# Decoder trunk with SwiGLU FFNs: the weight sums of the first FFN queued behind the latest activation split, and the second block's weight split queued behind the first block's copy

## The chip, the cores and the metric

The kernel runs on one core of a Trainium2 chip. The metric is the time of one execution on the device, in microseconds (us). The time before is the median of three runs, 1953.83 us (1948.05 to 1954.03). A profiled execution gives the trace from which all durations below come; its times are those of that one execution.

## What is computed

The reference is a decoder trunk of two layers on 512 tokens (T) of width 1024 (D). Each layer is a "macaron": half a feed-forward network (FFN), a token mixer (a short convolution in the first layer, sparse attention in the second), and another half FFN. That makes four FFNs. Cut to the part that the change touches:

```python
def swiglu(h, w_in, w_out):                 # h 512x1024, w_in 1024x(2*2816), w_out 2816x1024
    g, u = jnp.split(h @ w_in, 2, axis=-1)
    return (jax.nn.silu(g) * u) @ w_out

def adaln(x, g, shift, scale):
    return rms_norm(x, g) * (1 + scale[:, None, :]) + shift[:, None, :]

for i in range(DEPTH):
    mod = (cond @ ada_w[i] + ada_b[i]).reshape(bsz, 3, 3, D_MODEL)
    shift, scl, gate = mod[:, :, 0], mod[:, :, 1], mod[:, :, 2]
    h = adaln(x, norm_g[i, 0], shift[:, 0], scl[:, 0])
    x = x + HALF * gate[:, 0, None, :] * swiglu(h, ffn_w_in[i, 0], ffn_w_out[i, 0])
    ...
    h = adaln(x, norm_g[i, 2], shift[:, 2], scl[:, 2])
    x = x + HALF * gate[:, 2, None, :] * swiglu(h, ffn_w_in[i, 1], ffn_w_out[i, 1])
```

The products of the FFN are the bulk of the work. All data are float32.

## The kernel before

**A product in three.** TensorE multiplies in a shortened float32 form, so every operand is kept as two parts, high and low. `split` (L162) makes them: ScalarE copies the raw operand into the high part (L163), and VectorE subtracts that from the raw one to give the low part (L164). A product `mm3` is then three matmuls: high by high (L167), high weights by low data (L168 in the trace's names with `tl` or `hlo`), low weights by high data (L169, with `qal`, `wlo` and so on). A weight is usable when both its ScalarE copy and its VectorE subtraction are done, and each stands in the queue of its engine, which works in order.

**Seven products for eight.** The 2816 hidden units of an FFN are 22 blocks of 128, in four groups (`FOUR`: blocks 0 to 5, 6 to 11, 12 to 17, 18 to 21). For most blocks gate and up are computed together by `seven_products(j)`: a scheme that takes seven products of half size instead of eight, on sums of weight quarters and sums of data quarters. Each of the seven is 12 matmuls of 128x256. On TensorE a block reads its weights in this order: `a11` (tiles `whi`, `wlo`), then the `b4` product of the block before (`qdh`, `qdl`), `a12` (`whi`, `wlo`), `b2` (`qbh`, `qbl`), `s1` (`qah`, `qal`), the last product of the block before (`qch`, `qcl`), `s3` (`qah`, `qal`). The first block of a group has no block before it: `a11`, `a12`, `b2`, `s1`, `s3`. In the first FFN blocks 6 to 21 go this way (groups two to four), in the other three FFNs blocks 3 to 21.

**Where a block's weights come from.** Two loads by SyncE's queue (L647, L648) fill the halves of `qa`; an accumulating transfer of GpSimd's queue (L654) adds a third quarter to both. SyncE then loads `wraw` (L656) and `a22` (L657). VectorE forms the *weight sums*: L661 adds half of `wraw` to half of `qa`, L662 adds the other half of `wraw` to that; these give `qb` and so `b2` and `b4`. Then `split` makes `whi`/`wlo` from `wraw`, `qah`/`qal` from `qa`, and `qbh`/`qbl` from the first sum. In the first FFN there are two buffers for `qa`, three for `wraw`, `whi` and `wlo`, and one each for `qah`, `qal`, `qbh`, `qbl` and the rest; a load into a buffer waits until its last reader is done.

**After a product.** ScalarE copies the first three results out of PSUM into `e` and `e3` (L696, with raised priority); VectorE adds later products to them (L704, L713, L717); ScalarE applies Silu (L718); VectorE multiplies (L723, L724) to give the hidden activations `af`, and `split` makes `ahi` and `alo` of these. `hid.done` is the pair of instructions of the latest such split.

**Between groups.** After each group but an FFN's last, eight output projections (`y`) are added to `x` by VectorE (L804). In the first three FFNs VectorE also works through jobs for later sub-layers there: a row sum of the conditioning matrix (L147, on `adaraw`), whose 512 KB rows are loaded by GpSimd's queue (L153) or SyncE's. Some of these still stand in VectorE's queue when TensorE begins the next group.

**What sets the order.** Instructions are traced in the order of the code, and a scheduler orders each engine's queue by a priority that follows this order. Three context managers change it: `tc.high_priority()` moves an instruction forward, `behind(act, dve)` puts the instructions traced in it behind a given ScalarE and a given VectorE instruction of their queues, and `tc.issue_after(i)` puts them behind instruction `i`. A moved instruction keeps all that it waits for by data.

Of the kernel before, what the change touches and what calls it, by code (L numbers as in the profile page):

```python
# [16 lines left out]
AF = mybir.ActivationFunctionType  # L17
# [36 lines left out]
def decoder_kernel(ctx, tc, xT, cT, ng, adaw, adab, ffi, ffo, cwi, cw, cwo,  # L54
                   nwi, nwv, pos, w1, w2, qg, kg, nwo, rb, onehot, rowok, out):
    nc = tc.nc
# [20 lines left out]
    def psum(name, tag="mm"):  # L77
        tag = next(six) if tag == "mm" else {"pr": "o"}.get(tag, tag)
        return ps.tile([P, T], F32, name=name, tag=tag, bufs=2)
# [4 lines left out]
    def tmp(name, n=T, tag="t"):  # L84
        bufs, size = TAGS[tag]
        return tp.tile([P, n], F32, name=name, tag=tag, padded_shape=[P, size], bufs=bufs)
# [75 lines left out]
    def split(src, hi, lo):  # L162
        act = nc.scalar.activation(hi, src, AF.Copy)  # L163
        return act, nc.vector.tensor_tensor(lo, src, hi, ALU.subtract)  # L164

    def mm3(o, sh, sl, mh, ml, first, last, **kw):
        nc.tensor.matmul(o, sh, mh, start=first, stop=False, **kw)  # L167
        nc.tensor.matmul(o, sh, ml, start=False, stop=False, **kw)  # L168
        nc.tensor.matmul(o, sl, mh, start=False, stop=last, **kw)  # L169
# [61 lines left out]
    @contextmanager  # L231
    def behind(act, dve):
        with tc.issue_after(act.ins), tc.issue_after(dve.ins):
            yield
# [223 lines left out]
    class Hidden:  # L458
# [4 lines left out]
        def keep(self, af):  # L463
            hi = self.fa.tile([P, T], F32R, name="ahi", tag="a")
            lo = self.fa.tile([P, T], F32R, name="alo", tag="a")
            self.done = split(af, hi, lo)
            self.hi.append(hi)
            self.lo.append(lo)
# [151 lines left out]
    def ffn(s, f, nrm, nxt, w0, ahead, extra=(), soon=()):  # L620
        with ExitStack() as es:
            first = s == 0
# [5 lines left out]
            hid = Hidden(es, 12)  # L628
            keep = hid.keep
            nj = FOUR[0][1] if first else 2  # L630

            def seven_products(j, later, before):
                QT = KD * P // 2
                quart = lambda c, k: ffi[f, j, c].rearrange("p k n -> p (k n)")[:, k * QT:(k + 1) * QT]
                raw = wp.tile([P, 2, QT], F32, name="wraw", tag="wraw", bufs=3)
                whi = wp.tile([P, 2, QT], F32R, name="whi", tag="whi", bufs=3)
                wlo = wp.tile([P, 2, QT], F32R, name="wlo", tag="wlo", bufs=3)
                qa = next(sums)()  # L640
                a22 = tp.tile([P, T], F32, name="a22", tag="nacc", bufs=1) if j == nj and not first else tmp("a22")
                qb = [tmp("qb", tag="sq") for _ in range(2)] if first else swa.tile([P, 2, QT], F32, name="qb")
                qbs = qb if first else [qb[:, 0], qb[:, 1]]
                ah_, al_ = (sw.tile([P, 2, QT], F32R, name=f"qa{e}") for e in "hl")
                b2 = [sw.tile([P, QT], F32R, name=f"qb{e}") for e in "hl"]
                halves = qa if isinstance(qa, list) else [qa[:, 0], qa[:, 1]]
                nc.sync.dma_start(halves[0], quart(0, 0))  # L647
                nc.sync.dma_start(halves[1], quart(1, 1))  # L648
                a21 = quart(1, 0)
                if qa is halves:  # L650
                    for q in qa:
                        nc.gpsimd.dma_start(q, a21, accum_op=ALU.add)
                else:
                    nc.gpsimd.dma_start(qa, bass.AP(tensor=a21.tensor, offset=a21.offset, ap=[a21.ap[0], [0, 2], a21.ap[1]]),  # L654
                                        accum_op=ALU.add)
                nc.sync.dma_start(raw.rearrange("p a b -> p (a b)"), ffi[f, j, 0].rearrange("p k n -> p (k n)"))  # L656
                nc.sync.dma_start(a22, quart(1, 1))  # L657

                def operands(after):
                    with after():  # L660
                        nc.vector.tensor_tensor(qbs[0], halves[1], raw[:, 0], ALU.add)  # L661
                        nc.vector.tensor_tensor(qbs[1], qbs[0], raw[:, 1], ALU.add)  # L662
                    split(raw, whi, wlo)
                    if qa is halves:
                        for n, q in enumerate(qa):
                            split(q, ah_[:, n], al_[:, n])
                    else:
                        split(qa, ah_, al_)
                    split(qbs[0], *b2)

                if j == nj and first:
                    with behind(*held_back):
                        operands(nullcontext)
                elif later:
                    with behind(*hid.done):
                        operands(nullcontext)
                else:
                    operands((lambda: behind(*nrm.done[1])) if j == nj else nullcontext)

                def product(o, w, b, begin=True):  # L680
                    for i in range(KD // 2):
                        c = slice(i * P, (i + 1) * P)
                        mh, ml = b(i)
                        mm3(o, w[0][:, c], w[1][:, c], mh, ml, begin and i == 0, i == KD // 2 - 1, skip_group_check=True)

                a11, a12 = [(whi[:, i], wlo[:, i]) for i in range(2)]
                s3, s1 = [(ah_[:, i], al_[:, i]) for i in range(2)]
                t1, t2, t3, t4 = nrm.blocks
                lo, hi = slice(0, HT), slice(HT, T)
                ox, oy, oz = psum("gu"), psum("gu"), psum("gu")  # L690
                e = sw.tile([P, 2, HT], F32, name="e", bufs=2)
                e3 = tmp("e3", HT, "xr")

                def copied(to, o):
                    with tc.high_priority():
                        nc.scalar.activation(to, o[:, lo], AF.Copy)  # L696

                product(ox[:, lo], a11, nrm.quarter(0, 0))
                copied(e[:, 0], ox)
                before[0]()  # L700
                b4 = [sw.tile([P, QT], F32R, name=f"qd{e}") for e in "hl"]
                split(qbs[1], *b4)
                product(oz[:, lo], a12, nrm.quarter(1, 0))
                nc.vector.tensor_tensor(e[:, 0], oz[:, lo], e[:, 0], ALU.add)  # L704
                product(ox[:, lo], b2, t2, begin=False)
                copied(e[:, 1], ox)
                product(oy[:, lo], s1, t1)
                copied(e3, oy)
                before[1]()
                c22 = [sw.tile([P, QT], F32R, name=f"qc{e}") for e in "hl"]  # L710
                split(a22, *c22)
                product(ox[:, lo], s3, t3, begin=False)
                nc.vector.tensor_tensor(e3, ox[:, lo], e3, ALU.add)  # L713

                def fourth():
                    product(oy[:, lo], b4, nrm.quarter(1, 1), begin=False)
                    nc.vector.tensor_tensor(e[:, 1], oy[:, lo], e[:, 1], ALU.add)  # L717
                    nc.scalar.activation(e, e, AF.Silu)  # L718

                def last():  # L720
                    product(ox[:, lo], c22, t4, begin=False)
                    af = tmp("af")
                    nc.vector.scalar_tensor_tensor(af[:, hi], e[:, 1], -1.0, e3, op0=ALU.mult, op1=ALU.mult)  # L723
                    nc.vector.scalar_tensor_tensor(af[:, lo], e[:, 0], -1.0, ox[:, lo], op0=ALU.mult, op1=ALU.mult)  # L724
                    keep(af)

                return fourth, last

            js = [(j, c) for j in range(nj) for c in range(2)]
            shift(pool(es, "gap", 1, side="right"), 448)  # L730
# [7 lines left out]
            else:  # L738
                with ExitStack() as tf_es:
                    nrm.alloc_seven(hp, pool(tf_es, "tf", 1))  # L740
                    h = nrm.hi, nrm.lo
                    with ExitStack() as hw_es:
# [4 lines left out]
                        to = [tt.tile([P, D], F32R, name="w" + e, tag=f"t{e}1") for e in "hl"]  # L747
# [11 lines left out]
            if not first:  # L759
                for j in range(nj):  # L760
                    hid.activate(os[2 * j], os[2 * j + 1])
            held_back = []
            for p, (j0, j1) in enumerate(FOUR):
                rest = none = (lambda: None,) * 2
                for j in range(max(j0, nj), j1):
                    rest = seven_products(j, p and j == j0, rest)
                n = j1 - j0
                final = p == len(FOUR) - 1
                rest[0]()
# [11 lines left out]
                if not final:  # L781
                    begun = []
                    for d in range(KD):
                        if d < 2 and both:
# [11 lines left out]
                            w, o = begun[d]  # L796
                            project(o, w, 0, a, [(n - 1, n - 1)], False, True)
                        else:
# [3 lines left out]
                            o = psum("y")  # L802
# [10 lines left out]
            for i, d in enumerate(range(0, KD, 2)):  # L813
                if i < 2:
                    ws.append(ffn_out(f, d, 2, j0, j1))
                else:
                    t = (2, 0)[i - 2]
                    to = [tt.tile([P, KD // 2, HT], F32R, name=f"t{e}{t}").rearrange("p a b -> p (a b)") for e in "hl"]
                    raw = (own if first or i == 2 else quarter[0])().rearrange("p a b -> p (a b)")
# [18 lines left out]
            for d, t in [(d, 0) for d in range(6, KD)] + [(d, HT) for d in range(KD)]:  # L838
                o = psum("ty")
# [764 lines left out]
```

## Time and profile before

| what | value |
|---|---|
| median of the runs | 1953.83 us |
| the profiled execution | 1963.74 us |
| its span on the core | 1962.0 us |
| mean granted clock of TensorE | 0.990 |
| first FFN | about 19 to 412 us of the span |
| convolution mixer | 412 to 595 |
| second and third FFN | 600 to 941, 950 to 1290 |
| sparse attention | 1290 to 1620 |
| fourth FFN | 1630 to 1960 |

A page of the profile gives the busy time of each engine (PE is TensorE's matmuls, PEld its weight loads, DVE VectorE, ACT ScalarE, POOL GpSimd, SP SyncE), the span in slices, the transfers, and the chain of work that ended last. Views of the trace add to it: a timeline has one instruction a row (start, duration, engine, line, operation, out<-in, shapes; in brackets how long the engine stood idle before it and what ended that), the list of waits adds these up by what was waited for, and a table of windows gives busy times and the clock granted to TensorE in a stretch. A row's duration includes the end of a pipeline that overlaps the next instruction, so the spacing of two rows is often shorter than the first one's duration.

### The profile page before, as it was taken

To read this page: it belongs to the slowest core of one execution; us is meant where nothing else is said; L and a number is where in the kernel's file an instruction comes from. 1 tells how busy PE (TensorE), PEld (TensorE's weight loads), DVE (VectorE), ACT (ScalarE), POOL (GpSimd) and SP (SyncE) were. 2 spreads that over 40 slices of the span, in tenths; PEclk is the share of its full clock that TensorE was granted. 3 is DMA by queue.
4 is the path that set the end of the run, shared out by engine and by line. 5 is a ranking of instruction groups with operands and counts; after the bars stand their busy time and mean duration, and the time that the engine had idled before them with its cause. 6 is when DMAs were issued, how large, how long until landed. Compare 5 with 4: busy or idle time off the path is not lost.

```text
span 1962.0 us, 34451 instructions
## 1 busy us (share of the span) xinstructions
PE 1893.6 (97%) x13293; PEld 1756.4 (90%) x13293; DVE 1520.0 (77%) x2792; ACT 958.9 (49%) x1679; POOL 250.1 (13%) x346
## 2 busy tenths in 40 slices
PE   7998989899999999999999999999999999999999
PEld 5988888898889998989989898999989789898989
DVE  8966757679789787877968777788798988675765
ACT  3334343443226353535635353555688867363532
POOL 0010101000011111110011111000245531000100
PEclk9998999999999999999999999999999999999999
DMA  9575657528665676774377677324233324664741
GB/s 331 184 219 148 204 149 207 182 82 279 212 235 134 205 207 206 208 220 138 111 209 202 203 200 213 126 80 143 73 104 83 93 65 119 168 165 135 193 120 65
DMA packets 126673, 324.76 MB, mean 166 GB/s; under 512 B 15515, under 2 KB 16651, under 8 KB 126508
## 3 DMA queue, kind: packets, MB, share of 16 engines
q1 hardware_dynamic: 95196, 242.85, 37.4%
q0 software_dynamic: 31312, 79.71, 17.9%
q8 instruction: 104, 1.70, 0.3%
q14 instruction: 61, 0.50, 0.1%
HBM read 313.85 MB, written 3.15 MB: 162 GB/s over the span
## 4 chain that ended last, share of the span: by engine, by line
PE 65%; DVE 17%; DMA 10%; issue 4%; ACT 3%; SPq 1%; DVEq 0%; ACTq 0%; POOLq 0%
PE gu L167 11%; PE gu L169 10%; PE gu L168 10%; DMA wraw<-in_ffi 5%; PE y L167 4%; PE y L168 4%; PE y L169 4%; DMA qa<-in_ffi 4%; DVE wlo L164 3%; DVE adaraw L147 2%; PE cv L167 2%; PE cv L168 2%; PE cv L169 2%; PE ty L168 1%; PE ty L167 1%
## 5 line engine op out<-in xcount | busy, mean ns | idle before, releaser
L163 ACT ACTIVATE whi<-wraw 128x1024 fp32r<-128x1024 f32 (+2 forms) x261 | 252.8, 977 | 352.0 <-PE y L168 139.4
L164 DVE TENSOR_TENSOR wlo<-wraw,whi 128x1024 fp32r<-128x1024 f32 (+2 forms) x261 | 295.5, 1137 | 25.9 <-ACT whi L163 24.9
L168 PE MATMUL y<-alo,whi 128*128 128x512 f32 x576 | 224.4, 390 | 0.0
L167 PE MATMUL y<-ahi,whi 128*128 128x512 f32 x576 | 224.4, 390 | 0.0
L169 PE MATMUL y<-ahi,wlo 128*128 128x512 f32 x576 | 224.3, 389 | 0.0
L147 DVE CUSTOM_DVE_ANT_0 adaraw<-adaraw,cond,adabs 128x1024 f32<-128x1024 f32 x144 | 184.5, 1297 | 30.4 <-DMA adaraw<-in_adaw 30.2
L167 PE MATMUL gu<-hhi,whi 128*128 128x256 f32 x696 | 195.0, 280 | 0.0
L168 PE MATMUL gu<-hlo,whi 128*128 128x256 f32 x696 | 194.6, 280 | 0.0
L169 PE MATMUL gu<-hhi,wlo 128*128 128x256 f32 x696 | 194.5, 280 | 0.0
L169 PE MATMUL gu<-th,qal 128*128 128x256 f32 x584 | 165.9, 284 | 19.1 <-DVE qal L164 19.1
L167 PE MATMUL gu<-th,qah 128*128 128x256 f32 x584 | 165.9, 284 | 18.8 <-ACT e L696 18.8
L654 POOL DMA_DIRECT2D qa<-in_ffi x70 | 84.4, 1206 | 739.2 <-DMA qa<-in_ffi 176.0
L168 PE MATMUL gu<-tl,qah 128*128 128x256 f32 x584 | 164.7, 282 | 0.0
L167 PEld LDWEIGHTS gu<-hhi,whi 128*128 128x128 f32 x696 | 132.9, 191 | 0.7 <-DVE af L724 0.2
L168 PEld LDWEIGHTS gu<-hlo,whi 128*128 128x128 f32 x696 | 132.7, 191 | 0.5
L169 PEld LDWEIGHTS gu<-hhi,wlo 128*128 128x128 f32 x696 | 132.7, 191 | 0.0
L169 PEld LDWEIGHTS gu<-th,qal 128*128 128x128 f32 x584 | 113.2, 194 | 20.4 <-DVE qal L164 20.4
L167 PEld LDWEIGHTS gu<-th,qah 128*128 128x128 f32 x584 | 112.7, 193 | 20.8 <-ACT e L696 20.7
L169 PEld LDWEIGHTS y<-ahi,wlo 128*128 128x128 f32 x576 | 108.2, 188 | 22.9
L167 PEld LDWEIGHTS y<-ahi,whi 128*128 128x128 f32 x576 | 108.2, 188 | 21.6
L168 PEld LDWEIGHTS y<-alo,whi 128*128 128x128 f32 x576 | 108.1, 188 | 21.6
L696 ACT ACTIVATE e<-gu 128x256 f32<-128x256 f32 x219 | 81.0, 378 | 78.3 <-PE gu L169 78.2
(327 smaller groups left out, 5767.6 us busy)
## 6 DMA issues: line engine op xcount, KB each, us to landing
wraw<-in_ffi SPq DMA_DIRECT2D x103, 512.0 KB, 4.6
adaraw<-in_adaw POOLq DMA_DIRECT2D x79, 512.0 KB, 4.6
qa<-in_ffi SPq DMA_DIRECT2D x146, 256.0 KB, 3.8
wraw<-in_ffo SPq DMA_DIRECT2D x96, 384.0 KB, 3.8
qa<-in_ffi POOLq DMA_DIRECT2D x70, 512.0 KB, 7.1
adaraw<-in_adaw SPq DMA_DIRECT2D x65, 512.0 KB, 4.8
a<-in_ffi SPq DMA_DIRECT2D x73, 256.0 KB, 3.8
wraw<-in_cwi SPq DMA_DIRECT2D x24, 512.0 KB, 4.6
```

The source lines that it names most:

```text
L147: return nc.vector.tensor_tensor_reduce(out=raw, in0=raw, in1=cond, scale=scale, scalar=adabs[:, c:c + 1], op0=ALU.mult, op1=ALU.add, accu ...
L163: act = nc.scalar.activation(hi, src, AF.Copy)
L164: return act, nc.vector.tensor_tensor(lo, src, hi, ALU.subtract)
L167: nc.tensor.matmul(o, sh, mh, start=first, stop=False, **kw)
L168: nc.tensor.matmul(o, sh, ml, start=False, stop=False, **kw)
L169: nc.tensor.matmul(o, sl, mh, start=False, stop=last, **kw)
L654: nc.gpsimd.dma_start(qa, bass.AP(tensor=a21.tensor, offset=a21.offset, ap=[a21.ap[0], [0, 2], a21.ap[1]]), accum_op=ALU.add)
L696: nc.scalar.activation(to, o[:, lo], AF.Copy)
```

## The change

Two things are moved in `seven_products`; no instruction, tile or transfer is added or taken away.

1. In the first FFN, from its second block of this form on (`copied_before` is set), the weight sums L661 and L662 of block j are placed behind `hid.done`, the latest activation split traced so far: that of block j−2.
2. For the second block of each group, where a block of this form was traced before it in the same FFN, both parts of the split of `wraw` are placed behind ScalarE's second copy into `e` (after `b2`) of the block before, which is the first of its group.

```diff
-            def seven_products(j, later, before):
+            def seven_products(j, later, before, copied_before, second):
...
-                def operands(after):
-                    with after():
+                def operands(after=nullcontext):
+                    with after(), behind(*hid.done) if first and copied_before else nullcontext():
                         nc.vector.tensor_tensor(qbs[0], halves[1], raw[:, 0], ALU.add)
                         nc.vector.tensor_tensor(qbs[1], qbs[0], raw[:, 1], ALU.add)
-                    split(raw, whi, wlo)
+                    with tc.issue_after(copied_before.ins) if second else nullcontext():
+                        split(raw, whi, wlo)
...
-                copied(e[:, 1], ox)
+                copy = copied(e[:, 1], ox)
...
-                return fourth, last
+                return (fourth, last), copy
...
+            copy = None
             for p, (j0, j1) in enumerate(FOUR):
                 rest = none = (lambda: None,) * 2
                 for j in range(max(j0, nj), j1):
-                    rest = seven_products(j, p and j == j0, rest)
+                    rest, copy = seven_products(j, p and j == j0, rest, copy, copy and j == max(j0, nj) + 1)
```

`copied` now returns its instruction. Lines of the changed kernel are one higher behind L663 (L724 is L725 there), two higher from about L765 on (L804 is L806).

VectorE's queue in the first FFN, group two, around the activation split of block 6 (`alo`) before the change. L661 is that of block 9, `qal` that of block 8:

```order
L724 SCALAR_TENSOR_TENSOR af<-e,gu 128x256
L661 TENSOR_TENSOR qb<-qa,wraw 128x512
L164 TENSOR_TENSOR qcl<-a_1241,qch 128x512
L164 TENSOR_TENSOR alo<-af,ahi 128x512
L713 TENSOR_TENSOR e_1265<-gu,e_1265 128x256
L164 TENSOR_TENSOR qal<-qa,qah 128x1024
L717 TENSOR_TENSOR e<-gu,e 128x256
```

The same queue after the change, a block later: `alo` is block 7's, `qal`, L661 and L662 are block 9's, and `wlo` is block 11's. (`a_1376` is that block's `a22`, `e_1400` its `e3`.)

```order
L724 SCALAR_TENSOR_TENSOR af<-e,e_1265 128x256
L164 TENSOR_TENSOR wlo<-wraw,whi 128x1024
L725 SCALAR_TENSOR_TENSOR af<-e,gu 128x256
L164 TENSOR_TENSOR qcl<-a_1376,qch 128x512
L714 TENSOR_TENSOR e_1400<-gu,e_1400 128x256
L164 TENSOR_TENSOR qal<-qa,qah 128x1024
L164 TENSOR_TENSOR alo<-af,ahi 128x512
L661 TENSOR_TENSOR qb<-qa,wraw 128x512
L718 TENSOR_TENSOR e<-gu,e 128x256
L662 TENSOR_TENSOR qb<-qb,wraw 128x512
L164 TENSOR_TENSOR qbl<-qb,qbh 128x512
```

L661 stood ahead of `alo` and of the `qal` of the block before its own; now it stands behind `alo`, next to the `qal` of its own block, with L662 and `qbl` close behind.

VectorE's queue at the head of the second FFN's group two before the change; L147 are the last two row sums, L704 the first addition of the group's first block, and the `wlo` between the two row sums is that of the second block:

```order
L804 SCALAR_TENSOR_TENSOR x_85<-y,mods,x_85 128x512
L147 ISA adaraw,mods<-adaraw,cond,adabs,ngs 128x1024
L147 ISA mods 128x1
L164 TENSOR_TENSOR wlo<-wraw,whi 128x1024
L804 SCALAR_TENSOR_TENSOR x_85<-y,mods,x_85 128x512
L147 ISA adaraw,mods<-adaraw,cond,adabs,ngs 128x1024
L147 ISA mods 128x1
L164 TENSOR_TENSOR wlo<-wraw,whi 128x1024
L704 TENSOR_TENSOR e<-gu,e 128x256
L164 TENSOR_TENSOR wlo<-wraw,whi 128x1024
L164 TENSOR_TENSOR qbl<-qb,qbh 128x512
```

The same place after the change:

```order
L806 SCALAR_TENSOR_TENSOR x_85<-y,mods,x_85 128x512
L147 ISA adaraw,mods<-adaraw,cond,adabs,ngs 128x1024
L147 ISA mods 128x1
L806 SCALAR_TENSOR_TENSOR x_85<-y,mods,x_85 128x512
L147 ISA adaraw,mods<-adaraw,cond,adabs,ngs 128x1024
L147 ISA mods 128x1
L705 TENSOR_TENSOR e<-gu,e 128x256
L164 TENSOR_TENSOR qbl<-qb,qbh 128x512
L164 TENSOR_TENSOR wlo<-wraw,whi 128x1024
L714 TENSOR_TENSOR e_6896<-gu,e_6896 128x256
L164 TENSOR_TENSOR wlo<-wraw,whi 128x1024
```

The second block's `wlo`, and with it those of the blocks after it, moved from ahead of the last row sum to behind L705 and `qbl`. On ScalarE the copies into `e` come first there, and the `whi` of these blocks after them.

More of the change, by code (lines that the diff above doesn't have):

```diff
@@ L672, in seven_products @@
                     with behind(*held_back):
-                        operands(nullcontext)
+                        operands()
                 elif later:
                     with behind(*hid.done):
-                        operands(nullcontext)
+                        operands()
                 else:
@@ L695, in copied @@
                     with tc.high_priority():
-                        nc.scalar.activation(to, o[:, lo], AF.Copy)
+                        return nc.scalar.activation(to, o[:, lo], AF.Copy)
                 product(ox[:, lo], a11, nrm.quarter(0, 0))
```

## The prediction

> **What bounds the kernel now.** I read the page first, then PE's time in the groups of hidden blocks, then what PE waits for, then single rows around the waits.
>
> ```profile
> PE 1893.6 (97%) x13293; PEld 1756.4 (90%) x13293; DVE 1520.0 (77%) x2792; ACT 958.9 (49%) x1679; POOL 250.1 (13%) x346
> PE 65%; DVE 17%; DMA 10%; issue 4%; ACT 3%; SPq 1%; DVEq 0%; ACTq 0%; POOLq 0%
> ```
>
> PE (TensorE) is busy 97% of the span, and yet the chain that ended last runs 17% through VectorE (DVE) and 10% through transfers: there are places where PE waits, and "busy" hides more than it shows, as the next view tells. It is PE alone, one row for each group of hidden blocks in seven-product form: stretch and its length, PE busy and matmuls, granted clock, DMA share, GB/s. Three rows each for first, second, third and fourth FFN.
>
> ```profile
> 123.76:201.47 77.71, 67.78 (x517) 0.91 0.59 157
> 231.42:308.27 76.85, 66.73 (x517) 0.93 0.61 166
> 338.22:387.13 48.91, 41.36 (x338) 0.93 0.57 172
> 691.04:755.50 64.46, 61.94 (x517) 0.97 0.74 199
> 785.46:847.44 61.98, 60.34 (x518) 1.00 0.74 203
> 877.37:917.13 39.76, 38.81 (x337) 1.00 0.53 176
> 1037.61:1101.67 64.06, 61.94 (x517) 0.97 0.72 196
> 1131.63:1196.43 64.80, 62.06 (x517) 0.97 0.71 195
> 1226.36:1265.70 39.34, 38.81 (x338) 1.00 0.43 143
> 1717.10:1777.14 60.04, 60.04 (x517) 1.00 0.65 169
> 1807.07:1867.12 60.05, 60.05 (x518) 1.00 0.64 169
> 1897.05:1935.46 38.41, 38.41 (x337) 1.00 0.22 68
> ```
>
> The fourth FFN does the same matmuls without a wait, so its 60.04 and 38.41 us are the floor. Against it the first FFN loses 17.67, 16.81 and 10.50 (44.98), the second 4.42, 1.94 and 1.35 (7.71), the third 4.02, 4.76 and 0.93 (9.71): **62.4 us** in all. The waits of PE in the stretch 120 to 390 us, which holds the first FFN's three groups (us in total, times, longest), and then from 600 to 1300, which holds the next two FFNs:
>
> ```profile
> PE gu L169 <- DVE qal L164: 19.1, 7, 5.1
> PE gu L167 <- ACT e L696: 8.5, 4, 3.5
> ...
> PE gu L167 <- ACT e L696: 11.2, 7, 2.7
> ```
>
> The waits make 38.8 us, of which 0.7 lies at 991 us outside the groups. The other 24.3 of the 62.4 is clock:
>
> ```profile
> 153.25 0.39 PE L169 MATMUL gu<-th,qal 128*128 128x256 f32 x1 [1.86 <-DVE qal L164]
> 153.20:155.70 2.50, 2.45 (x16) 0.77 0.52 138
> 155.70:158.00 2.30, 2.30 (x13) 0.51 0.92 287
> 792.82 0.39 PE L167 MATMUL gu<-th,qah 128*128 128x256 f32 x1 [1.64 <-ACT e L696]
> 793.00:795.00 2.00, 2.00 (x19) 1.00 0.73 231
> ```
>
> A wait of 1.86 us is followed by two microseconds and more at half clock; a wait of 1.64 is not. Eleven waits of these twelve groups are above 1.8 us and one more lies at 1.64, so 24.3 over eleven, 2.2 us each, is the most that a wait costs beyond itself. The second FFN's last two groups lose only 0.3 and 0.4 beyond their waits; with that much taken off for the groups a trip to half clock costs about **2.0 us**, the value I use.
>
> [...]
>
> **Part one: the weight sums of the first FFN.** Why does PE wait for `qal`? DVE's queue around the first such wait, then the transfers:
>
> ```profile
> 149.84 0.69 DVE L661 TENSOR_TENSOR qb<-qa,wraw 128x512 f32<-128x512 f32 x1 [5.02 <-DMA qa<-in_ffi]
> ...
> 151.05 0.68 DVE L164 TENSOR_TENSOR alo<-af,ahi 128x512 fp32r<-128x512 f32 x1
> 151.65 0.42 DVE L713 TENSOR_TENSOR e<-gu,e 128x256 f32<-128x256 f32 x1
> 151.98 1.22 DVE L164 TENSOR_TENSOR qal<-qa,qah 128x1024 fp32r<-128x1024 f32 x1
> ...
> 153.22 0.33 SPq L647 DMA_DIRECT2D qa<-in_ffi  x1
> ...
> 164.29 0.69 DVE L661 TENSOR_TENSOR qb<-qa,wraw 128x512 f32<-128x512 f32 x1 [5.83 <-DMA qa<-in_ffi]
> ```
>
> `qal` of block 8 stands behind the sum L661 of block 9, which idles DVE for 5.02 us until POOL's accumulating transfer onto block 9's `qa` has landed. And that `qa` buffer's next load is issued as soon as `qal` has read the other one (153.22), POOL then adds to it, and the next L661 goes at 164.29. So one loop holds a transfer, an accumulation and a split: 164.29 − 149.84 = 14.45 us here, of which each block needs one; a block's seven products take seven times 1.36 us, 9.5 us, on PE (product starts are quoted below). With two buffers the loop could serve two blocks at a time, 19 us, but queue order ties `qal` of one to the landing of the other.
>
> The change puts L661 and L662 of block j behind `alo` of block j−2, next to `qal` of the same block j, where `qa(j)` must have landed anyway. `qal(j)` then waits only for its own transfer, and the loop has two block periods, 19 us, for its 14.5: 4.5 us to spare. So all seven `qal` waits go: **19.1 us**, and six of them, all but one of 0.85 us, are above 1.8, so 6 × 2.0 = **12.0 us** of clock. No instruction is added or removed; POOL's queue keeps its order, and SP's loads of `wraw` that wait for the later sums move behind loads of `qa`.
>
> What is late next: the sums themselves. Between the end of the sixth product of a block (which `alo` comes from) and `b2` of the next but one block lie four products on PE, 4 × 1.36 = 5.4 us. After it stand, in rows:
>
> ```profile
> 194.78 0.42 DVE L724 SCALAR_TENSOR_TENSOR af<-e,gu 128x256 f32<-128x256 f32 x1 [2.35 <-PE gu L169]
> ...
> 195.99 0.68 DVE L164 TENSOR_TENSOR alo<-af,ahi 128x512 fp32r<-128x512 f32 x1
> ```
>
> From L724 to the end of `alo` 1.9 us, then L713 0.35, L661 0.6, `qal` 1.15 by the spacings in the fence before, and L662 and `qbl`, of the same size as L661, 0.6 and 0.7, 5.3 us. That is as long as the four products: a block can lose nothing to 0.35 us at `b2`. In groups two and three one more thing is in the way at the second and third block after the head (9 and 10, 15 and 16): a split for later work stands ahead in DVE's queue (block 11's `wlo`, then one of the output projections' weights), and its load, on SP, waits for an L662 that is now later. For block 9 I add up to 1.7 us, for block 10 1.45. Bounds: from 0.35 each, if that load lands in time, to 2 us more each, if the load meets the other transfers (DMA share 0.92 in the row at 155.70). I take the sums as they come from durations, below the clock's trip: 0.35 + 1.7 + 1.45 + 0.35 = 3.85 for each of the two groups, **7.7 us** given back. Group four has two blocks of this kind and gives about 0.5, inside the rounding.
>
> **Part two: the heads of the groups.** The second FFN's head at 691 us:
>
> ```profile
> 693.87 0.28 PE L167 MATMUL gu<-th,qbh 128*128 128x256 f32 x1
> 695.23 0.28 PE L167 MATMUL gu<-th,qah 128*128 128x256 f32 x1
> ...
> 697.37 1.06 ACT L163 ACTIVATE whi<-wraw 128x1024 fp32r<-128x1024 f32 x1 [4.33 <-DMA wraw<-in_ffi]
> ...
> 697.11 1.34 DVE L147 CUSTOM_DVE_ANT_0 adaraw<-adaraw,cond,adabs 128x1024 f32<-128x1024 f32 x1 [2.25 <-DMA adaraw<-in_adaw]
> 698.38 1.22 DVE L164 TENSOR_TENSOR wlo<-wraw,whi 128x1024 fp32r<-128x1024 f32 x1
> 699.52 0.41 DVE L704 TENSOR_TENSOR e<-gu,e 128x256 f32<-128x256 f32 x1
> ```
>
> Products start 1.36 us apart (693.87, 695.23). ScalarE (ACT) copies `e` only after a split that waited 4.33 us for its weights; PE waits 2.52 us for that copy. After the change the copy comes first and this wait goes. But the second block's `wlo`, so far done before the last row sum L147, moves behind it: behind L147 (1.27 to the next start), L704 (0.33) and `qbl` (0.60), and takes 1.22 itself. Its end is then 697.11 + 3.43 = 700.54. PE needs it two products and two matmuls after 695.23, at 695.23 + 2 × 1.36 + 0.23 = 698.18. So PE waits **2.36** there, in the next block's first product, for what it saved before it. L147 starts when its transfer lands, which the change does not touch. The other seven heads with row sums, done alike from the starts of L147 and of the fourth product (the first and the last of the eight):
>
> ```profile
> 237.68 1.28 DVE L147 CUSTOM_DVE_ANT_0 adaraw<-adaraw,cond,adabs 128x1024 f32<-128x1024 f32 x1 [2.49 <-DMA adaraw<-in_adaw]
> 1230.44 1.28 DVE L147 CUSTOM_DVE_ANT_0 adaraw<-adaraw,cond,adabs 128x1024 f32<-128x1024 f32 x1 [2.52 <-DMA adaraw<-in_adaw]
> ```
>
> The waits come out, for the first FFN's groups three and four, at 2.55 and 3.7 (before 2.64 and 0.92 + 1.50); second FFN 2.36, 1.49, 0.67 (before 2.52, 1.64, 0.95); third 1.52, 2.58, 0.37 (before 2.12, 2.74, 0.53). Together 15.2 for 15.6, with four trips to half clock before and four after: **0.4 us gained**, nothing more. Bounds: if `wlo` still hides, all 15.6 and four trips go, 23.6; if L147 comes 1 us later, 8 and some clock are lost, about 12.
>
> One head is free of this: the first FFN's second group, whose last row sum is over before the head and whose wait for the copy was the longest, 3.5 us in the list above. It goes with its trip: **5.5 us**. The heads of group one in the later FFNs have no row sum and 0.7 us to win; the fourth FFN waits nowhere and may lose about 0.5 by the later split. These I set against each other.
>
> **The sum.** 19.1 + 12.0 + 5.5 + 0.4 − 7.7 = **29.3 us** gained, 29 for short. Against the profiled execution, 1963.74, that gives 1934.7; that execution was 0.5% above the median of the runs, 1953.83, so for the time I take 1953.83 − 29 = **1925**. A measurement of this kernel can tell some 0.3%, 5.9 us, from no change.
>
> **The rivals.** *The heads clear too.* The load in this SP row goes into the buffer that the second block's split gave back. After the change it is issued some 6 us later, and the row sum's transfer could have its share:
>
> ```profile
> 694.22 0.33 SPq L656 DMA_DIRECT2D wraw<-in_ffi  x1
> 690.00:697.00 7.00, 6.75 (x54) 6.36 (x52) 4.83 (x7) 1.44 (x2) 0.53 (x1) 1.00 1.03 293
> ```
>
> The engines are full from 690 to 697 (share 1.03). If the row sum's transfer (POOL's queue) shared them with that load for the 2.9 us until 697.11 it lands up to 1.45 us earlier: the eight waits shrink to 1.1, 2.25, 0.9, 0, 0, 0.1, 1.1, 0, that is by 9.8, and three trips go, 6. Time 1925 − 16 = **1909**. Against it: `whi` at 697.37 waited for an earlier load of the same SP queue until then, so that queue had work to 697 in any case. [...] Chance 0.12.
>
> *The sums are late.* The load behind L662 lands later and blocks 9, 10, 15 and 16 wait some 2 us more each, across the bound of the clock: 4 × (1 to 2 + 2.0) is 12 to 16 us. Time **1937 to 1941**; up to 1945 if group four joins. Chance 0.15.
>
> *The loop still binds,* since accumulations land as late as before and `qal` waits for its own `qa`: what part one gives is lost, and the time stays within 0.3%, about **1954**. The 4.5 us to spare speak against it. Chance 0.06.
>
> *Slower.* The sums' chain has no slack (5.3 of 5.4 us). If the accumulating transfer of a block lands more than 7 us later in the loop (4.5 to spare and 2.4), L661 starts that much late and PE waits at `b2` in each of the ten blocks 8 to 11, 14 to 17, 20 and 21: 10 × (2.4 + 2.0) = 44 us in place of my 7.7 brings **1961**, slower than before. It decides from about 2.4 us of lateness a block; below that it is faster. The longest accumulation seen before lands well below that. Chance 0.06.
>
> **How the numbers follow.** Forecast 0.61 (1915 to 1934), heads clear 0.12, sums late 0.15, loop binds 0.06, slower 0.06. Faster by over 0.3%: 0.61 + 0.12 + 0.15 = 0.88; within: 0.06; slower: 0.06. The range 1906 to 1943 takes in the first three nearly whole.
>
> **What would show it.** Right: no wait for `qal` in the first FFN; L661 never idle for `qa` ahead of `alo`; the first FFN's groups at about 64, 69 and 44 us; at the eight heads a wait of L169 for `wlo` in the next block's first product, 0.4 to 3.7 us, in place of that for `e`; short waits at `b2` of blocks 9, 10, 15, 16. Wrong: waits for `qal` or L661 with long idles for `qa`; heads without a wait; `b2` waits at every block, or with half clock behind them.

## The result, and the profile after

The changed kernel takes **1931.76 us** (median of four runs, 1928.02 to 1934.63) against 1951.97 for the kernel before beside it (median of four): a ratio of 0.990, 95% interval 0.987 to 0.992. A second set gave 1930.71 us against 1956.22 beside it, 0.987 (0.985 to 0.989). That is faster by about 1%, inside the range of 1906 to 1943, and 7 us behind the 1925 that were forecast. Each ratio in this document is taken against runs of the kernel before in the same set; the sets ran on several chips, with medians of the kernel before from 1951.97 to 1956.71 us, so times of different sets are compared less safely than ratios. Profile against profile the change is larger: the span goes from 1962.0 to 1931.3 us, the profiled execution from 1963.74 to 1933.05 us. The forecast for that was 1934.7.

The page's engine busy times and its chain of work that ended last:

```profile
PE 1881.0 (97%) x13293; PEld 1742.4 (90%) x13293; DVE 1515.2 (78%) x2792; ACT 950.9 (49%) x1679; POOL 250.6 (13%) x346
PE 74%; DVE 13%; DMA 7%; ACT 3%; issue 3%; SPq 1%; POOL 0%; DVEq 0%; ACTq 0%; POOLq 0%
```

PE's part of the chain rises from 65% to 74%; VectorE's and the transfers' fall. PE's busy time falls by 12.6 us with the same 13293 matmuls: this is read as half clock that is gone, since the mean granted clock rises from 0.990 to 0.998. PE in the same twelve groups (length, busy and matmuls, granted clock, DMA share, GB/s), in the order of the prediction's table:

```profile
124.89:189.62 64.73, 61.78 (x517) 1.00 0.71 193
219.56:289.14 69.58, 62.98 (x517) 0.98 0.69 185
319.07:358.02 38.95, 38.76 (x337) 1.00 0.66 203
661.71:725.52 63.81, 62.00 (x518) 0.97 0.76 200
755.47:818.54 63.07, 60.36 (x518) 1.00 0.76 202
848.48:887.62 39.14, 38.87 (x338) 1.00 0.56 179
1008.40:1070.09 61.69, 60.38 (x518) 1.00 0.75 202
1100.10:1161.66 61.56, 60.64 (x518) 1.00 0.76 203
1191.59:1231.62 40.03, 38.71 (x338) 1.00 0.45 147
1684.77:1745.32 60.55, 60.36 (x518) 1.00 0.66 170
1775.25:1835.90 60.65, 60.46 (x517) 1.00 0.66 170
1865.83:1904.79 38.96, 38.77 (x338) 1.00 0.23 69
```

Against the floor of 60.04 and 38.41 us the first FFN's groups now lose 4.7, 9.5 and 0.5, 14.8 us where it was 45.0; the second FFN 7.5 (7.7 before), the third 4.8 (9.7), and the fourth, which had lost nothing, 1.7. The first FFN is the source of nearly all of the gain. Its waits from 120 to 390 us, then those of the next two FFNs from 580 to 1300 (us in total, times, longest):

```profile
PE gu L169 <- DVE wlo L164: 4.6, 3, 4.2
PE gu L167 <- DVE af L725: 2.8, 2, 1.5
PE gu L169 <- DVE qbl L164: 2.3, 2, 1.2
...
PE gu L169 <- DVE wlo L164: 8.5, 7, 2.7
```

The seven waits for `qal` (19.1 us) and those for `e` are gone; in place of the latter stand waits for `wlo`. VectorE's queue shows why `qal` is free (first FFN, group two; with one load of SP's queue and one copy of ScalarE; L661, `qal` and L662 are block 8's, the load, `whi` and `wlo` block 11's, and the last row is block 7's last multiply):

```profile
142.23 0.69 DVE L164 TENSOR_TENSOR alo<-af,ahi 128x512 fp32r<-128x512 f32 x1
...
143.17 0.69 DVE L661 TENSOR_TENSOR qb<-qa,wraw 128x512 f32<-128x512 f32 x1
143.77 1.22 DVE L164 TENSOR_TENSOR qal<-qa,qah 128x1024 fp32r<-128x1024 f32 x1
144.90 0.69 DVE L662 TENSOR_TENSOR qb<-qb,wraw 128x512 f32<-128x512 f32 x1
...
145.92 0.38 SPq L656 DMA_DIRECT2D wraw<-in_ffi  x1
...
150.92 1.06 ACT L163 ACTIVATE whi<-wraw 128x1024 fp32r<-128x1024 f32 x1 [1.31 <-DMA wraw<-in_ffi]
...
152.02 1.23 DVE L164 TENSOR_TENSOR wlo<-wraw,whi 128x1024 fp32r<-128x1024 f32 x1 [4.22 <-ACT whi L163]
153.16 0.41 DVE L725 SCALAR_TENSOR_TENSOR af<-e,gu 128x256 f32<-128x256 f32 x1
```

L661 runs behind `alo` and one addition without an idle gap; `qal` follows at once. The groups by operation say the same for the whole program: idle time before L661, first before, then after:

```profile
L661 DVE TENSOR_TENSOR qb<-qa,wraw 128x512 f32<-128x512 f32 x73 | 50.0, 685 | 66.4 <-DMA qa<-in_ffi 35.5 <-DMA wraw<-in_ffi 19.6 <-issue 9.7
```

```profile
L661 DVE TENSOR_TENSOR qb<-qa,wraw 128x512 f32<-128x512 f32 x73 | 50.1, 687 | 21.1 <-DMA wraw<-in_ffi 18.7 <-issue 2.4
```

VectorE no longer stands still ahead of L661 for a transfer into `qa` (35.5 us before, none listed now). What it stands still for now is `wlo` at 152.02, whose weights load late: 4.22 us. The load goes out at 145.92, after L662 (144.90) has read the buffer that it goes into, and ScalarE waits for it until 150.92. Behind `wlo` stands the multiply L725 that frees the PSUM tile of the next `a11`; PE loses 1.48 us there.

The heads of the groups, where `wlo` follows the last row sum:

```profile
227.65 1.28 DVE L147 CUSTOM_DVE_ANT_0 adaraw<-adaraw,cond,adabs 128x1024 f32<-128x1024 f32 x1 [3.60 <-DMA adaraw<-in_adaw]
...
228.86 0.42 DVE L705 TENSOR_TENSOR e<-gu,e 128x256 f32<-128x256 f32 x1
229.19 0.68 DVE L164 TENSOR_TENSOR qbl<-qb,qbh 128x512 fp32r<-128x512 f32 x1
229.79 1.22 DVE L164 TENSOR_TENSOR wlo<-wraw,whi 128x1024 fp32r<-128x1024 f32 x1
...
231.06 0.38 PE L169 MATMUL gu<-hhi,wlo 128*128 128x256 f32 x1 [4.21 <-DVE wlo L164]
```

The chain is the one that was forecast, in its order and its length: from the start of L147 to PE's first matmul on `wlo` 231.06 − 227.65 = 3.41 us here, and 3.4 to 3.5 at the other heads.

### The profile page after: what moved, and what is told of

It is laid out like the page before. It is cut to its first block, busy times and chain, and to the rows that moved or that the text cites. A ratio compares the mean times of both kernels' runs of the same rounds, so it can differ in the third digit from the quotient of the medians.

```text
span 1931.3 us, 34417 instructions
## 1 busy us (share of the span) xinstructions
PE 1881.0 (97%) x13293; PEld 1742.4 (90%) x13293; DVE 1515.2 (78%) x2792; ACT 950.9 (49%) x1679; POOL 250.6 (13%) x346
## 4 chain that ended last, share of the span: by engine, by line
PE 74%; DVE 13%; DMA 7%; ACT 3%; issue 3%; SPq 1%; POOL 0%; DVEq 0%; ACTq 0%; POOLq 0%
PE gu L169 11%; PE gu L167 11%; PE gu L168 11%; PE y L167 5%; PE y L169 5%; PE y L168 5%; DMA adaraw<-in_adaw 2%; DVE wlo L164 2%; PE cv L167 2%; PE cv L168 2%; PE cv L169 2%; DMA wraw<-in_ffi 2%; PE ty L168 2%; PE ty L167 2%; PE ty L169 2%
## 5 line engine op out<-in xcount | busy, mean ns | idle before, releaser
L147 DVE CUSTOM_DVE_ANT_0 adaraw<-adaraw,cond,adabs 128x1024 f32<-128x1024 f32 x144 | 185.2, 1303 | 40.3 <-DMA adaraw<-in_adaw 40.1
L167 PE MATMUL gu<-th,qah 128*128 128x256 f32 x584 | 161.4, 276 | 0.8 <-ACT e L697 0.8
L169 PE MATMUL gu<-th,qal 128*128 128x256 f32 x584 | 161.3, 276 | 0.0
```

Of the source, the lines that this page charges most:

```text
L147: return nc.vector.tensor_tensor_reduce(out=raw, in0=raw, in1=cond, scale=scale, scalar=adabs[:, c:c + 1], op0=ALU.mult, op1=ALU.add, accu ...
```

## The experiments

**The kernel before, once more.** No edit.

> The kernel before, once more, to see how much of its loss recurs. If the profiled execution of before was an ordinary one, the span is again about 1962 us, with 19 us of waits for qal and 20 us for e in all. If it was a long one (its 1963.74 stand 12 us above the median of its runs, 1951.97), the span is near 1950 and the 12 us are missing from waits for qal or from half clock behind them.

Measured: 1955.0 us (1943.99 to 1956.71, ten runs), ratio 0.999 (0.997 to 1.000); the 23 runs of before in that set lie between 1947.56 and 1963.35, median 1956.17. The profiled span is 1953.9. Its waits, 120 to 390 and then 580 to 1300:

```profile
PE gu L169 <- DVE qal L164: 19.8, 7, 3.5
PE gu L167 <- ACT e L696: 10.2, 3, 5.2
...
PE gu L167 <- ACT e L696: 5.8, 6, 1.7
```

Neither expectation was right as it stood: `qal` costs the same, and what is smaller is the wait for `e` at the heads of the two later FFNs (5.8 us, 11.2 in the first profile) with the clock behind it (mean granted clock of the execution 0.992, 0.990 in the first profile); in the first FFN that wait is larger (10.2 us, 8.5 before). The twelve groups lose 56.3 us here, 62.4 in the profile that the forecast was made from: 6.1 of the 8.1 us between the two spans. Of the 56.3, 48.2 are in the first FFN (45.0 in the first profile) and 8.1 in the second and third (17.4). The execution at 1963.74 was longer than any of those 23.

**Part one alone.**

```diff
-  rest, copy = seven_products(j, p and j == j0, rest, copy, copy and j == max(j0, nj) + 1)
+  rest, copy = seven_products(j, p and j == j0, rest, copy, False)
```

> Part one alone: the weight sums of the first FFN behind the latest activation split, the weight splits where they were before. Theory (part one carries the gain, part two only trades one wait at the heads for another): no wait for qal in the first FFN, the short waits for af and qbl at blocks 9, 10, 15, 16 (5 us) stay, the waits for e at the nine heads come back with about 19 us, the waits for wlo there (12.5 us) go, as do those of the fourth FFN (3 us); about 1936 us, ratio 0.992. Rival (the two parts need each other, or part two gives most): ratio 0.996 or more.

Measured: 1931.91 us (1927.18 to 1937.1), ratio **0.987** (0.985 to 0.989). No wait for `qal`; the waits, by the same two windows:

```profile
PE gu L167 <- ACT e L697: 8.1, 3, 4.4
PE gu L167 <- DVE af L725: 3.6, 2, 1.9
...
PE gu L167 <- ACT e L697: 12.6, 6, 3.6
```

Part one carries the whole gain: 1931.9 against 1931.8 and 1930.7 for both parts. The waits for `e` are back, 20.7 us in a profiled execution that is the longest of the five, and nothing can be seen lost by it in the median. The theory had put this kernel at 1936 and 0.992, 4 us too high and above the interval; that part one carries the gain stands, and the rival's 0.996 falls.

**Part two alone.**

```diff
-  with after(), behind(*hid.done) if first and copied_before else nullcontext():
+  with after():
```

> Part two alone: the second blocks' weight splits behind the copy, the weight sums where they were before. Theory: the waits for qal stay with 15 to 19 us and their half clock; at the heads the waits for e become waits for wlo of 10 to 15 us; only the first FFN's second group gains (about 5 us) and the fourth FFN loses about 3: 1945 to 1952 us, ratio 0.997 to 1.000. Rival (part two gives most): 1940 or less.

Measured: 1953.49 us (1947.88 to 1958.56), ratio 0.998 (0.997 to 1.000), no difference that can be told. `qal` waits 16.2 us in seven waits, `wlo` 5.4 us in the first FFN and 8.0 in the next two, and no wait for `e` is listed there. As expected: part two trades one wait for another.

**The last row sum out of the head.** The job of the eighth output projection goes into the next group's fourth block.

```diff
+  pend = []
...
+  if pend and j == j0 + 3:
+      pend.clear()
+      with tc.issue_after(hid.done[1].ins):
+          each()
   rest, copy = seven_products(...)
...
-  if p or not first or 2 <= d < KD - 1:
+  if d == KD - 1 and (p or not first):
+      pend.append(1)
+  elif p or not first or 2 <= d < KD - 1:
```

> The changed kernel with the last row sum of each head (the one of the eighth output projection) moved into the fourth block of the next group, behind the latest activation split. Theory (wlo waits at the heads only because it stands behind a row sum whose transfer lands late): the seven waits for wlo in the first three FFNs, 12.5 us, and two trips to half clock, 4 us, go, and under 2 us come back in the middle of the groups: about 1917 us, ratio 0.982. Rival (wlo is late for another reason, its own load or the queue behind the copy): the waits stay within 3 us of what they are, and the time at 1929 to 1934.

Measured: **1921.33 us** (1918.54 to 1922.02), ratio 0.982 (0.980 to 0.984). The waits for `wlo` from 580 to 1300 us:

```profile
PE gu L169 <- DVE wlo L164: 1.3, 7, 0.2
```

8.5 us have become 1.3, 0.2 at each head, and in the second and third FFN nothing comes back in the middle of the groups, which take 60.6 and 39.0 us: the moved row sum starts there about 27.5 us after its group, and VectorE does not idle before it. The theory holds. The median is 4 us above its 1917; the 0.5 us that each group of the second to fourth FFN still loses is about that much, and the last experiment returns to it.

**The same, without part two.** Its edit is those of part one alone and of the moved row sums together.

> Part one and the moved row sums, without part two: does the split behind the copy matter once the last row sum is out of the head? Theory (two independent causes stand at each head, the copy behind a split that waits for its load and the split behind a row sum that waits for its row; part two takes away the first and exposes the second): the waits for e stay with 8 to 20 us in all and some half clock, about 1928 us (1924 to 1933), so that part two is worth some 7 us here and nothing alone. Rival (the row sums were the only cause): the waits for e go too and the time is that of the moved row sums with part two, 1921 within 2 us.

Measured: 1935.57 us (1927.08 to 1941.68), ratio 0.989 (0.986 to 0.992). The waits for `e` stay, 3.7 us in the first FFN and 9.5 in the next two. The row below them is ScalarE at the head of the second FFN's group two, where the copies into `e` follow this split and PE waits 2.68 us for them:

```profile
PE gu L167 <- ACT e L697: 3.7, 3, 2.3
...
PE gu L167 <- ACT e L697: 9.5, 7, 2.7
...
668.59 1.06 ACT L163 ACTIVATE whi<-wraw 128x1024 fp32r<-128x1024 f32 x1 [4.50 <-DMA wraw<-in_ffi]
```

The rival falls. The time is above the theory's range of 1924 to 1933; the profiled execution is the fastest of the four, 8 us under the median, so that the median run loses more than these rows show, where is not known. So two causes stand side by side at the heads, and either alone holds PE: moving the row sum without part two gains nothing (0.989 beside 0.987 for part one alone), part two without moving the row sum gains nothing (0.987 with both parts), both together gain 10 us.

**One buffer for `qa`.**

```diff
-  own = partial(swa.tile, [P, 2, KD * P // 2], F32, name="qa", bufs=1 + first)
+  own = partial(swa.tile, [P, 2, KD * P // 2], F32, name="qa", bufs=1)
```

> The changed kernel with one buffer for qa in the first FFN in place of two. Theory (the loop of qal, load, accumulation and split takes 13 to 14.5 us, and the new order hides it only because two buffers give it two blocks' time): the loop binds at each of some 13 blocks, 4 to 5 us more a block than TensorE's 9.5, with long waits for qal or qah; 1975 to 2000 us. Rival (the transfers were short all along, the old waits came from queue order alone): 1945 or less.

Measured: 1975.8 us in one run, 45 us slower than the changed kernel; nearly all of it is in the first FFN, whose three groups take 79.43, 82.60 and 55.43 us, 44 us more than with two buffers. The three largest waits from 115 to 400 us, and two rows of VectorE:

```profile
PE gu L167 <- ACT qbh L163: 9.9, 5, 3.2
PE gu L169 <- DVE qbl L164: 8.5, 8, 1.2
PE gu L169 <- DVE wlo L164: 6.9, 3, 3.6
...
172.86 0.69 DVE L661 TENSOR_TENSOR qb<-qa,wraw 128x512 f32<-128x512 f32 x1 [1.06 <-DMA qa<-in_ffi]
...
187.09 0.69 DVE L661 TENSOR_TENSOR qb<-qa,wraw 128x512 f32<-128x512 f32 x1 [2.51 <-DMA qa<-in_ffi]
```

The loop of split, load and accumulation is as long as was said: the two L661 of neighbouring blocks, which both wait for `qa`, start 14.2 us apart. The second buffer is what the new order uses. The place was missed: the waits are at `b2`, for the sums, not at `s1` for `qal`, since the sums now come first in the queue.

**The late weight splits of the first FFN.** On top of the moved row sums; `qd[0]` is the VectorE half of the latest `b4` split.

```diff
-  with tc.issue_after(copied_before.ins) if second else nullcontext():
+  with tc.issue_after(copied_before.ins) if second else tc.issue_after(qd[0].ins) if first and qd and j > 8 else nullcontext():
       split(raw, whi, wlo)
...
-  split(qbs[1], *b4)
+  qd[:] = [split(qbs[1], *b4)[1]]
...
-  begun.append((ffn_out(f, dd, 1, j0, j1), psum("y")))
+  begun.append((weights(ffo[f, dd:dd + 1, :, j0 * P:j1 * P].rearrange("d p c -> p d c"), j1 - j0, P, after=qd[0] if first else None), psum("y")))
```

> The moved row sums, and in the first FFN the weight splits of blocks 9 to 11 (15 to 17, 21) and those of the first two output projections behind the b4 split of the block before. Theory (the last multiply of a block, which frees the PSUM tile for a11, stood behind a weight split that waited for its load): the waits for af, qbl and qbh in the first FFN, 6 us, go: about 1915 us (1912 to 1918). Rival (the chain of alo, sums and qbl is too long by itself): qbl waits stay, 1919 or more.

Measured: 1922.73 us (1920.81 to 1926.9), ratio 0.983 (0.981 to 0.985): no gain over 0.982. Waits from 115 to 400 us:

```profile
PE gu L169 <- DVE qbl L164: 2.9, 4, 1.2
PE y L169 <- DVE wlo L164: 2.7, 2, 1.5
PE gu L167 <- ACT qbh L163: 2.3, 2, 1.2
PE gu L167 <- DVE af L725: 1.0, 1, 1.0
```

The expectation missed. `af` does free itself (2.9 us in the kernel it builds on, 1.0 here), but `qbl` and `qbh` wait as much as before or more and the output projections' own `wlo` is now late. The rival's reading fits: the chain from `alo` over the sums to `qbl` has no slack. That was not measured apart from the rest.

**Part two only where it pays,** on top of the last one. `extra` holds the jobs for later sub-layers, of which the fourth FFN has none:

```diff
-  copy and j == max(j0, nj) + 1)
+  bool(extra) and (p or first) and copy and j == max(j0, nj) + 1)
```

> The one before, with part two left out where no row sum or split stood in the way: group one and the whole fourth FFN. Theory: the 0.2 us waits for wlo and 0.3 to 1.5 us more at seven heads go, about 4 us: 1911 us (1908 to 1914). Rival (those heads cost nothing): equal to the one before within 1.5 us.

Measured: 1918.2 us (1918.04 to 1922.06), ratio 0.981 (0.979 to 0.983), 4.5 us under the kernel it builds on, as the theory has it, though the two sets of runs overlap; the 1911 built on the 1915 that had not come.

**The changed kernel once more,** beside the last one. No edit.

> The changed kernel once more, beside the next one on the same chip: 1929 to 1935 us, ratio 0.987 to 0.990; its waits for wlo at the seven heads again follow the start of the last row sum.

Measured: 1930.71 us (1925.41 to 1937.24), ratio 0.987 (0.985 to 0.989). The heads again follow the row sum: the last L147 starts 4.5 to 6.3 us after the group (3.9 to 8.1 in the first profile), and the longest wait for `wlo` (2.41 us) stands behind the latest of them.

**The moved row sums, and part two only where it pays.** The edit of the moved row sums with the one just shown.

> The moved row sums alone, with part two left out in group one and in the fourth FFN. Theory (part two only pays where a split that waits for its load stands ahead of the copy; elsewhere it costs 0.5 us a head and up to 2.6): the fourth FFN's groups are back at 60.04, 60.05 and 38.4 us and the time is 4 us under that of the moved row sums alone, 1917 us (1914 to 1919), ratio 0.980. Rival (noise of those heads): 1920 to 1923.

Measured: **1916.8 us** (1915.78 to 1917.89), ratio **0.980** (0.978 to 0.982), the fastest kernel of this study, 14 us under the changed one beside it and 4.5 under the moved row sums alone, with no overlap of their runs (on two chips). A group of the second and one of the fourth FFN:

```profile
660.60:721.17 60.57, 60.38 (x518) 1.00 0.75 205
...
1670.78:1730.83 60.05, 60.05 (x518) 1.00 0.65 170
```

The fourth FFN is back at its floor, and the second and third are 0.5 above it in their long groups.

## Why the prediction was right, and where its size was off

**Part one.** Right in mechanism and in size. All seven waits for `qal` and the half clock behind them went (forecast 19.1 + 12.0 us; the three groups' granted clock was 0.91 to 0.93 and is 0.98 to 1.00), and with the head of group two they make the first FFN's loss fall by 30 us in the profiles. Part one alone gives the whole measured gain, and one buffer in place of two takes it back and more, so the loop of `qa`, served over two blocks, is shown. (The prediction's sentence on the buffers reads the rows in the wrong order: the load at 153.22 is block 10's and goes into the buffer that `qal` of block 8 had just read. The 14.45 us of the loop are not touched by that.)

**What it gives back.** 7.7 us forecast; 1.5 and 1.3 at `a11` and 1.2 and 1.1 at `b2` measured, 5.0 us (5.4 in the second profile). The cause was named, a later split ahead in VectorE's queue whose load waits for a later L662, but block 9 stops one step earlier than was said: not at `b2` but at `a11`, whose PSUM tile L725 frees. The 0.35 us at the other blocks did not show.

**The heads.** Forecast: nothing but an exchange, 15.2 us for 15.6. Measured: 12.7 us of `wlo` waits (4.2, 0.2, 1.8, 2.7, 0.3, 1.3, 0.9, 1.3), two half clocks in place of four (granted clock 0.50 at 233.00 to 235.00 us, behind the wait of 4.2, and at 672.80 to 674.80, behind that of 1.8). The chain behind L147 took the 3.43 us that were worked out. What differed is where each L147 starts, which the forecast took over from the trace of before: 6.26 us after its group's start became 8.09, and 7.52 became 3.93. It also moves between two executions of one kernel: at the last of these it is 7.52 and 5.28 in the two profiles of before, 3.93 and 6.03 in the two of the changed kernel. So a single head can't be forecast from a single trace; the first FFN's last group, put at 44 us, took 38.95 in one profile and 42.82 in the other. That part two alone gives 0.998, and part one without it the whole 0.987, fits the exchange.

**The cost of the new order at other heads.** The fourth FFN was put at 0.5 us. It is 4.3 in the first profile: 0.5 or 0.6 at each of three heads and 2.6 in group one (0.8 between the second profiles of the two kernels), and leaving part two out there gave some 4 us back. Mis-sized, and it was set against the 0.7 us of the other group ones, which did not come either (0.3 and 0.4 lost, by the second profiles 0.5 and 0.9).

**From profile to median.** This is the step that failed. The sum, −29.3 us, met the profiles (1934.7 forecast, 1933.05 measured); subtracted from the median of the runs it gave 1925, and 1931.76 came. The medians fell by 20.2 us in the first set and 25.5 in the second, less than 29 in both. The forecast took the 10 us by which the profiled execution of before stood above its median as something that the change would leave alone. The second profiles show otherwise. What the groups lose against the floor, in us:

| profile | first FFN | second | third | fourth |
|---|---|---|---|---|
| before | 45.0 | 7.7 | 9.7 | 0 |
| before, once more | 48.2 | 4.6 | 3.6 | 0 |
| changed | 14.8 | 7.5 | 4.8 | 1.7 |
| changed, once more | 16.5 | 5.7 | 5.2 | 1.8 |

The gain in the first FFN, 30 to 32 us, comes back in both pairs. The second and third FFN lost 17.4 us in the execution that the forecast was made from and 8.1 in the other; the changed kernel loses 12.3 and 10.9 there. The even exchange of the forecast, taken apart, is a gain of 3.5 us at these six heads (waits of 10.5 against 9.0, and a half clock less at the estimated 2.0 us) and a loss of 3.2 at the two of the first FFN. At the six heads one pair of profiles shows a gain of 5 us, the other, taken on two chips, a loss of 3. With the 4 to 5 us that the fourth FFN and the group ones cost, the pairs come out at 30 and 25 us; the spans fall by 30.7 and 23.7.

As an estimate, the forecast's remaining losses, 62.4 − 29.3 = 33.1, set against the 56.3 of the second profile give −23, and 1931. That the sum met the first pair so closely is in part luck: the first FFN gained 30.2 where the sum comes to 25.7 (19.1 + 12.0 + 5.5 − 7.7 less the 3.2), the later heads 5.1 where it comes to 3.5, and 5.0 us of cost that it set at nothing took that back. The small set adds to the miss: 1953.83 is the median of three runs, and the later sets have medians of 1956.2 to 1956.7.

**The rivals.** That the sums come late enough to bring half clock with them did not happen (the four waits are 1.1 to 1.5 us, and the granted clock in the 3.5 to 4.4 us behind each is 1.00). The loop no longer binds: there is no wait for `qal`. The heads did not clear on their own, though two of the eight came out under 0.3 us; they clear when the row sum is moved. Whether a row sum's transfer lands earlier once the load beside it is gone was not measured apart.

## What to carry to other kernels

An instruction that waits for a slow transfer (VectorE stood still 5.02 and 5.83 us ahead of two L661 of the kernel before) belongs, in an in-order queue, behind everything that is ready before it; here one move of that kind, with no work saved, gave about 1%. Where a wait is only exchanged for another, look for the second cause and take both away: at these heads neither part two nor the moved row sum gained anything alone, and together they gained 10 us. And before a loss that is seen in one profiled execution is subtracted from a median, see how far that execution stands above the median, and profile a second one to learn which of the losses recur.

## What was not expected of the hardware

Half clock does not follow from the length of a wait alone. In the changed kernel a wait of 1.81 us is followed by half clock and one of 2.71 is not (nor is one of 2.80 us in the second profile of before, at 169.42); the rows of the two waits, then the clock behind them:

```profile
670.82 0.38 PE L169 MATMUL gu<-hhi,wlo 128*128 128x256 f32 x1 [1.81 <-DVE wlo L164]
...
765.48 0.39 PE L169 MATMUL gu<-hhi,wlo 128*128 128x256 f32 x1 [2.71 <-DVE wlo L164]
```

```profile
670.80:672.80 2.00, 1.99 (x13) 0.79 0.67 238
672.80:674.80 2.00, 2.00 (x12) 0.50 0.88 246
...
765.40:767.40 2.00, 1.92 (x16) 1.00 0.84 270
767.40:769.40 2.00, 2.00 (x20) 1.00 0.70 232
```

Taking a trip for every wait above 1.8 us fitted the trace of before (behind each of its eleven waits of 1.86 to 5.14 us in the groups the granted clock is 0.50 to 0.68 over the next 3.5 to 4.8 us, behind those of 0.53 to 1.64 us it is 1.00) and overstated these. What decides between them stays open.
